# Moving the rotary part of the queries, its tables and the key rotation from the attention's start into the last column pair of the input projection (hybrid encoder, one core)

## The chip, the cores and the metric

One core of a Trainium2 chip runs the whole program. The metric is the device time of one execution in microseconds (us). The kernel before takes 1529.16 us, the median of three runs from 1528.39 to 1529.31.

## The reference

Two layers. Each normalises its input (512 positions of width 2048), projects it with one matrix `w_in`, and splits the result into three groups of heads and a gate. Cut to what matters here:

```python
cos, sin = rope_tables(positions)
for l in range(DEPTH):
    z = rmsnorm(x, pre_norm_g[l]) @ w_in[l]
    q_lat, kv_lat, k_pe, gb, gc, xin, q_mem, gate = split_cols(z)
    q = (rmsnorm(q_lat, q_norm_g[l]) @ w_uq[l]).reshape(b, s, 8, 192)
    q = concat([q[..., :128], apply_rope(q[..., 128:], cos, sin)], -1)
    k_pe = apply_rope(k_pe, cos, sin)                  # one key rotation, shared by the heads
    a_out = mla_attention(q, concat([k_nope, k_pe]), v)
    c_out = short_gated_conv(gb, gc, xin, conv_w[l])
    mem_n = rmsnorm(mem, mem_norm_g[l])                # 256 memory tokens
    m_out = memory_attention(q_mem, mem_n, w_mk[l], w_mv[l])
    y = concat([a_out, c_out, m_out], -1) * silu(gate)
    x = x + rmsnorm(y @ w_o[l], post_norm_g[l])
```

## The kernel before

Every product is made of three TensorE (PE) passes over a high and a low part of both operands (`mm3`, lines 243 to 247: L245, L246 and L247 are its three matmuls). So each block of weights that is loaded into a raw tile `wr` is first split: ScalarE (ACT) rounds it into `wh` (L172, or L177 with a gain), VectorE (DVE) takes the rest as `wl` (L173 or L178). What leaves PE and is to be multiplied again is split the same way by `split_to` (ACT L250, DVE L251). Raw tiles come from a pool of 8 buffers, `wh` and `wl` from 3 each, PSUM banks from 8, wide tiles ("slabs") from 19.

`Program` holds a list of steps. The order on PE, SyncE (SP, which issues the loads) and GpSimd (POOL, which issues accumulating loads) is the order of that list. The order on DVE and ACT is fixed at build time by a scheduler that starts from the same list. Each engine then runs its own list strictly in order; semaphores connect them. `pr.defer` puts a piece off until the steps have room for it.

A layer goes through these stages:

- The input projection, as five groups of two column blocks each (`gs[0]` to `gs[4]`), each group with seven products P1 to P7 in place of eight. A group's steps are four long (`c` = 0 to 3) per product. Between them stand small steps, such as `conv_turn`. Group 3 makes the latents (`lat`); group 4, the last, makes the gate columns `ga0` and `ga1`. Its 28 steps run P1, P5 with P2, P6 with P3, P7, P4.
- Within group 4: `latents_begin` normalises the latents, `latent_turn` transposes them (`cq`, `ckv`), `qm_turn` the memory queries (`Qm`), `gate_turn` the gate columns `gm` (a transpose on PE into a bank `tps`, then SiLU on ACT, L742). In layer 0 also `mem_rows` (L646): for each of two halves of the memory an ACT sum of squares over 128x2048 (L536), two small POOL operations for the root (L255, L257) and a DVE scaling (L544) give `mhs`.
- `mixer` (L1031). Layer 0: eight times `mem_turn` (PE transposes `mhs` into a bank `mps`, L660; ACT and DVE split it into `mH` and `mL`) alternates with the eight gate turns of `ga0` and `ga1` and with the memory keys and values (`mem_steps`: `mk` 24 matmuls of 256 columns and `mv` 12 of 512 columns for each of eight row pairs). The rotary tables (`tables`, L299, ropescr) and the key rotation (`k_rope`, L789) are deferred pieces beside these. Layer 1 fetches its memory keys and values, which were made earlier, and does the eight gate turns.
- Then the rotary part of the queries (`q_rope_steps`, L830): two product steps `prods` of 24 matmuls into four banks `qr`, whose weights are loaded from `w_uq` in pieces of 64 columns; four steps `rot`, each four DVE products against the tables (L856, L858), one DVE sum (L860) and one split into `qs`; four steps `turn`, each eight transposes on PE (`qrt`, L879) and two ACT copies into `QR` (L881). In layer 0 the products stand after the memory values, in layer 1 among the gate turns. `rot` and `turn` stand among the first steps of the attention.
- The attention as a software pipeline (L1011): scores (`sc`) on PE, maximum on DVE (L956), exponential and scaling on ACT (L959, L962), transposes `ptp` (L973), product with the values (`o`). First the four memory heads (their keys and values are `Km` and `Vm`), with the query, key and value projections of the first two heads (`qps`, `kps`, `vps`) between them; then the eight latent heads in pairs. The output projection follows.

Of the kernel before, what the change touches and what calls it, by code (L numbers as in the profile page):

```python
# [5 lines left out]
F32 = mybir.dt.float32  # L6
# [6 lines left out]
P = 128  # L13
# [64 lines left out]
class Program:  # L78
# [19 lines left out]
    def add(self, fn, units=(), room=0.0, ahead=None):  # L98

        self.steps.append((list(units), fn, room, self.ahead if ahead is None else ahead))  # L100
# [100 lines left out]
def encoder(tc, x, mem, positions, pre_norm_g, w_in, q_norm_g, w_uq, kv_norm_g, w_ukv, conv_w,  # L201
# [32 lines left out]
    def slab(name, dt=F32):  # L234
        return slabs.tile([P, D], dt, tag="slab", name=nm(name))
# [63 lines left out]
    def tables():  # L299
        n = NT * HALF  # L300
        v = {}

        def begin():
            v["scr"] = slab("ropescr").rearrange("p (i n) -> p i n", n=n)
            pf = const.tile([P, NT], F32, name="posf")
            nc.vector.tensor_copy(pf, G["posi"])
            ang, a2, tot = (v["scr"][:, i, :] for i in (0, 1, 4))
            for t in range(NT):
                nc.vector.tensor_scalar_mul(ang[:, t * HALF:(t + 1) * HALF], G["inv"], pf[:, t:t + 1])
            v["a1"] = scrap("ra1", n, F32R)  # L310
            nc.vector.tensor_copy(v["a1"], ang)
            nc.vector.tensor_tensor(a2, ang, v["a1"].bitcast(F32), op=ALU.subtract)
            v["ti"] = scrap("rti", n, I32)
            nc.vector.memset(tot, 0.0)

        def term(hi, part):
            def g():
                a2, f, tot = (v["scr"][:, i, :] for i in (1, 3, 4))
                a = v["a1"].bitcast(F32) if hi else a2
                nc.vector.tensor_scalar_mul(v["ti"], a, part)  # L320
                nc.vector.scalar_tensor_tensor(f, a, part, v["ti"], op0=ALU.mult, op1=ALU.subtract)
                nc.vector.tensor_tensor(tot, tot, f, op=ALU.add)
            return g

        def wave(shift):
            def g():
                q, f, tot, c = (v["scr"][:, i, :] for i in (2, 3, 4, 5))
                name = "cos2" if shift else "sin2"
                dst = G[name] = const.tile([P, NT, 2, HALF], F32, name=name)
                src = tot  # L330
                if shift:
                    nc.vector.tensor_scalar_add(q, tot, shift)
                    src = q
                nc.vector.tensor_scalar(f, src, MAGIC, None, op0=ALU.add)
                nc.vector.tensor_scalar(f, f, MAGIC, None, op0=ALU.subtract)
                nc.vector.tensor_tensor(f, src, f, op=ALU.subtract)
                nc.vector.tensor_scalar_mul(f, f, TWO_PI)
                nc.vector.tensor_scalar(f, f, PI_DOWN, -PI_DOWN, op0=ALU.min, op1=ALU.max)
                nc.scalar.activation(c, f, AF.Sin)
                c3 = c.rearrange("p (t i) -> p t i", i=HALF)  # L340
                if shift:
                    nc.vector.tensor_copy(dst[:, :, 0, :], c3)
                else:
                    nc.vector.tensor_scalar_mul(dst[:, :, 0, :], c3, -1.0)
                nc.vector.tensor_copy(dst[:, :, 1, :], c3)
            return g

        parts = inv_two_pi_parts(5)
        pr.defer(1.4, begin)
        for k in range(4, -1, -1):  # L350
            for hi in (False, True):
                pr.defer(0.8, term(hi, parts[k]))
        pr.defer(1.6, wave(0.0))
        pr.defer(1.8, wave(0.25))
# [673 lines left out]
            out.setdefault(int(n * start + k * n * (1 - start) / len(steps)), []).append(s)  # L1028
        return out

    def mixer(l, C, gates, pair2, tail):  # L1031

        prods, rot, turn = q_rope_steps(l)
        if l == 0:
            ms = [(f, u, 1.0) for f, u, _ in mem_steps(l)]
            add(tables)
            add(lambda: pr.defer(3.5, lambda: k_rope(C)))
            for q in range(8):
                add(lambda q=q: mem_turn(q))
                add(gates[q])  # L1040
                if q:
                    put(ms[2 * q - 2:2 * q])
            put(ms[14:])
            add(pr.settle)
            add(k_rope_turn)
            put(prods)
        else:
            add(mem_fetch)
            put([(g, []) for g in gates[:4]], prods[:1], [(g, []) for g in gates[4:]], prods[1:])
        sts = [{} for _ in range(4)]  # L1050
        qkv = qkv_steps(l, 0, sts[0])
        add(*rot[0])
        fill = []
        for t in range(NT):
            fill += [qkv[t]] + ([rot[t + 1]] if t + 1 < NT else []) + [turn[t]]
        its = [it for i in range(4) for it in mem_head(i)]
        m = len(its)
        between = spread(m, fill + qkv[4:])
        for pair in range(4):
            for i in range(2):  # L1060
                its += mla_head(2 * pair + i, sts[pair])
            nxt = tail if pair == 3 else spread(6 if pair == 2 else 8, qkv_steps(l, pair + 1, sts[pair + 1]))
            if pair == 2:
                nxt.update(pair2)
            for k, v in nxt.items():
                between[m + 8 * pair + k] = v
        pipeline(its, between)
# [144 lines left out]
    for l in range(depth):  # L1212
# [57 lines left out]
        put(a1, b1)  # L1270
        put(*gs[0][2:], *gs[1][2:])
        add(owns[2])
        put(gs[2][0])
        conv = [(conv_turn(l, c, C), []) for c in range(4)]
        put(weave(gs[2][1] + gs[2][2], conv, 2), *gs[2][3:])
        add(owns[3])
        put(*gs[3])
        add(owns[4])
        add(lambda l=l: latents_rows(l))
        if l == 0:  # L1280
            add(positions_load)
        g4 = [s for steps in gs[4] for s in steps]
        put(g4[:4])
        add(lambda l=l, C=C: latents_begin(l, C))
        put(g4[4:8])
        if l > 0:
            add(lambda C=C: k_rope(C))
        put(g4[8:16])
        if l == 0:
            add(mem_load)  # L1290
            G["mTd"] = dram.tile([4, P, D], F32, name="mTd")
        lat = [latent_turn("cq", j) for j in range(4)] + [latent_turn("ckv", j) for j in range(2)] + [k_rope_turn] * (l > 0)
        gm = lambda t, C=C: C["gm"][:, t, :]
        more = [(f, []) for f in lat + [qm_turn(j, C) for j in range(4)] + [gate_turn(12 + j, gm, j) for j in range(4)]]
        if l == 0:
            more.insert(8, (mem_rows, []))
        put(weave(g4[16:], more[:11], 1))
        put(more[11:])
        gates = [gate_turn(j, lambda t, C=C, j=j: C["ga0" if j < 4 else "ga1"][:, t, :], j % 4) for j in range(8)]
        G["left"] = Y = Left(False)  # L1300
        g0, g1, gains, fetch = out_proj(l)
# [7 lines left out]
        def sums(p):  # L1309
            def f():  # L1310
# [6 lines left out]

        last_pair = {0: [(sums(0), []), g0[0][0]], 1: [g0[0][1]], 2: [g0[0][2]], 3: [g0[0][3]],
                     4: [g1[0][0]], 5: [g1[0][1]], 6: [g1[0][2]], 7: [g1[0][3]]}
        mixer(l, C, gates, {6: [(use_y, []), (low(0), [])], 7: [(low(1), [])]}, last_pair)  # L1320
        add(sums(1))
        add(gains(0))
        put(*g0[1:])
# [47 lines left out]
```

## Time and profile before

| what | value |
|---|---|
| median of 3 runs | 1529.16 us |
| the profiled execution | 1529.26 us |
| its span, first to last instruction | 1527.5 us |
| mean granted TensorE clock | 0.994 |
| PE matmuls / PE weight loads busy | 98% / 84% of the span |
| DVE / ACT / POOL busy | 68% / 57% / 21% of the span |

The profile's times are of one execution, which the hardware profiler took. Some 1.8 us of its time lie outside the span. "Idle before" is the time that an engine stood still just before an instruction, with the instruction that released it. The ends of matmuls are modelled, since they overlap; the distance between two starts is the better measure of what a matmul costs.

### The profile page before, as it was taken

The numbers are of one execution on the slowest core, as the hardware profiler recorded it, in microseconds if no ns is written. First come the engines' busy times: TensorE is split into PE (matmuls) and PEld (weight loads), VectorE is DVE, ScalarE is ACT, GpSimd is POOL, SyncE is SP. The second block draws the span as 40 slices with busy tenths as digits, with TensorE's granted clock in tenths as the row PEclk, the third lists the DMA queues.
The fourth block names the chain that finished last, engine by engine and source line by source line (L and its number), as shares of the span: only waits on it lengthen the run. The fifth ranks groups of instructions, "written<-read, shape, count | busy, mean of one in ns | idle before, by whom it ended". The sixth has DMA issues, their size and how long they took to land.

```text
span 1527.5 us, 20239 instructions
## 1 busy us (share of the span) xinstructions
PE 1493.4 (98%) x7613; PEld 1281.3 (84%) x7613; DVE 1040.1 (68%) x1398; ACT 864.7 (57%) x1335; POOL 314.9 (21%) x313
## 2 busy tenths in 40 slices
PE   9999999999999999999999999999999999999996
PEld 7888888988898888888788888888988888888884
DVE  6965675565968668865778766675566586687656
ACT  7733534454768768645578434434454686775542
POOL 1233131332000000324320333131332000003231
PEclk9999999999999999999999999999999999999998
DMA  8999898989581112699997999897989411048895
GB/s 330 216 213 224 204 174 174 199 196 256 164 264 56 42 42 82 109 202 197 313 332 239 238 224 226 187 176 168 198 207 222 130 59 39 29 111 146 203 200 222
DMA packets 146934, 275.59 MB, mean 180 GB/s; under 512 B 17340, under 2 KB 40212, under 8 KB 143508
## 3 DMA queue, kind: packets, MB, share of 16 engines
q0 software_dynamic: 65600, 141.57, 48.5%
q1 hardware_dynamic: 81104, 132.68, 26.7%
q8 instruction: 59, 0.97, 0.3%
q14 instruction: 39, 0.32, 0.1%
q10 hardware_dynamic: 132, 0.05, 0.0%
HBM read 259.59 MB, written 14.68 MB: 180 GB/s over the span
## 4 chain that ended last, share of the span: by engine, by line
PE 85%; DVE 4%; DMA 3%; issue 3%; ACT 3%; POOL 2%; POOLq 0%; DVEq 0%; ACTq 0%
PE P L246 20%; PE P L247 20%; PE P L245 19%; PE ptp L973 2%; PE tps L731 1%; DMA mL<-mTd 1%; PE o L246 1%; PE sc L245 1%; PE mk L246 1%; PE sc L246 1%; PE sc L247 1%; PE mk L247 1%; PE o L247 1%; PE o L245 1%; DVE wl L173 1%
## 5 line engine op out<-in xcount | busy, mean ns | idle before, releaser
L173 DVE TENSOR_TENSOR wl<-wr,wh 128x1024 fp32r<-128x1024 f32 (+1 forms) x408 | 486.4, 1196 | 334.6 <-ACT wh L172 332.2
L172 ACT CAST wh<-wr 128x1024 fp32r<-128x1024 f32 (+1 forms) x408 | 420.6, 1033 | 482.5 <-PE P L247 418.2
L246 PE MATMUL P<-wl,S 128*128 128x512 f32 (+1 forms) x896 | 344.2, 384 | 2.8 <-DVE wl L173 2.8
L245 PE MATMUL P<-wh,S 128*128 128x512 f32 (+1 forms) x896 | 346.0, 386 | 0.0
L247 PE MATMUL P<-wh,S 128*128 128x512 f32 (+1 forms) x896 | 343.4, 383 | 0.0
L134 POOL DMA_DIRECT2D wr<-in_w_in_dram x160 | 193.4, 1209 | 484.5 <-DVE wl L173 365.2
L246 PE MATMUL P<-wl,A 128*128 128x512 f32 (+1 forms) x656 | 251.9, 384 | 2.1 <-DVE wl L173 2.1
L245 PE MATMUL P<-wh,A 128*128 128x512 f32 (+1 forms) x656 | 253.1, 386 | 0.2 <-ACT wh L172 0.2
L247 PE MATMUL P<-wh,A 128*128 128x512 f32 (+1 forms) x656 | 251.6, 384 | 0.5 <-DVE A L251 0.5
L246 PEld LDWEIGHTS P<-wl,S 128*128 128x128 f32 x896 | 168.3, 188 | 33.7 <-DVE wl L173 4.4
L247 PEld LDWEIGHTS P<-wh,S 128*128 128x128 f32 x896 | 168.2, 188 | 30.4
L245 PEld LDWEIGHTS P<-wh,S 128*128 128x128 f32 x896 | 168.1, 188 | 29.6 <-ACT wh L172 0.2
L134 POOL DMA_DIRECT2D wr<-in_w_o_dram x64 | 77.3, 1208 | 505.0 <-DVE rec L961 352.0
L246 PEld LDWEIGHTS P<-wl,A 128*128 128x128 f32 x656 | 123.2, 188 | 24.4 <-DVE wl L173 2.9
L247 PEld LDWEIGHTS P<-wh,A 128*128 128x128 f32 x656 | 123.1, 188 | 23.3 <-DVE A L251 1.2
L245 PEld LDWEIGHTS P<-wh,A 128*128 128x128 f32 x656 | 123.1, 188 | 22.3 <-ACT wh L172 0.6
L959 ACT ACTIVATE P<-sc,nm 128x512 f32<-128x512 f32 (+1 forms) x96 | 59.9, 624 | 36.4 <-DVE nm L956 35.8
L962 ACT ACTIVATE P<-P,rec 128x512 f32<-128x512 f32 (+1 forms) x96 | 62.1, 658 | 5.0 <-DVE rec L961 5.0
L956 DVE TENSOR_REDUCE nm<-sc 128x1 f32<-128x512 f32 (+1 forms) x96 | 57.2, 596 | 10.0 <-PE sc L954 6.3
L251 DVE TENSOR_TENSOR PT<-ptp,PT 128x512 fp32r<-128x512 f32 (+1 forms) x96 | 56.5, 594 | 8.5 <-ACT PT L250 8.1
L178 DVE SCALAR_TENSOR_TENSOR wl<-wr,cols,wh 128x512 fp32r<-128x512 f32 x64 | 46.2, 747 | 18.2 <-ACT wh L177 18.0
L177 ACT ACTIVATE wh<-wr,cols 128x512 fp32r<-128x512 f32 x64 | 44.2, 722 | 25.2 <-PE mk L246 10.9
(267 smaller groups left out, 2182.4 us busy)
## 6 DMA issues: line engine op xcount, KB each, us to landing
wr<-in_w_in_dram POOLq DMA_DIRECT2D x128, 512.0 KB, 6.9
wr<-in_w_in_dram SPq DMA_DIRECT2D x112, 512.0 KB, 5.6
wr<-in_w_o_dram POOLq DMA_DIRECT2D x64, 512.0 KB, 7.3
wr<-in_w_o_dram SPq DMA_DIRECT2D x48, 512.0 KB, 3.9
wr<-in_w_in_dram POOLq DMA_DIRECT2D x32, 416.0 KB, 5.4
wr<-in_w_in_dram SPq DMA_DIRECT2D x24, 416.0 KB, 4.3
wr<-in_w_mk_dram SPq DMA_DIRECT2D x16, 512.0 KB, 6.9
wr<-in_w_mv_dram SPq DMA_DIRECT2D x16, 512.0 KB, 4.5
```

The source lines that it names most:

```text
L134: engine.dma_start(dst, src, **kw)
L172: nc.scalar.copy(hi[:, :n], src)
L173: nc.vector.tensor_tensor(lo[:, :n], src, hi[:, :n].bitcast(F32), op=ALU.subtract)
L177: nc.scalar.activation(hi[:, h], src[:, h], AF.Copy, scale=g)
L178: nc.vector.scalar_tensor_tensor(lo[:, h], src[:, h], g, hi[:, h].bitcast(F32), op0=ALU.mult, op1=ALU.subtract)
L245: nc.tensor.matmul(ps, ah, bh, start=first, stop=False, **kw)
L246: nc.tensor.matmul(ps, ah, bl, start=False, stop=False, **kw)
L247: nc.tensor.matmul(ps, al, bh, start=False, stop=last, **kw)
L251: nc.vector.tensor_tensor(lo, src, hi.bitcast(F32), op=ALU.subtract)
L956: nc.vector.tensor_reduce(nmax, ps, axis=AX.X, op=ALU.max, negate=True)
L959: nc.scalar.activation(pt, ps, AF.Exp, bias=nmax, accum_out=tot)
L962: nc.scalar.activation(pt, pt, AF.Copy, scale=rec)
```

## The change

- The two products `prods` of the rotary queries now stand around the last step of P7 of group 4, the four `rot` steps between the steps of P4 and after them, alternating with the turns of the memory queries. Only `turn` stays in the attention.
- The tables are built beside group 3 in layer 0, from `positions` loaded one group earlier. The table's scratch is a raw tile now, no slab.
- The key rotation of layer 0 stands within group 4, as that of layer 1 did already; its transposes stand among the latent turns.
- In layer 0 `mem_rows`, which was put among the small steps before the gate turns of `gm`, is appended behind them.

```diff
@@ tables
-            v["scr"] = slab("ropescr").rearrange("p (i n) -> p i n", n=n)
+            v["scr"] = raw_p.tile([P, 1024], F32, tag="raw", name="ropescr")[:, :6 * n].rearrange("p (i n) -> p i n", n=n)
@@ mixer
-    def mixer(l, C, gates, pair2, tail):
-        prods, rot, turn = q_rope_steps(l)
+    def mixer(l, gates, turn, pair2, tail):
         if l == 0:
             ms = [(f, u, 1.0) for f, u, _ in mem_steps(l)]
-            add(tables)
-            add(lambda: pr.defer(3.5, lambda: k_rope(C)))
             for q in range(8):
                 add(lambda q=q: mem_turn(q))
                 add(gates[q])
                 if q:
                     put(ms[2 * q - 2:2 * q])
             put(ms[14:])
-            add(pr.settle)
-            add(k_rope_turn)
-            put(prods)
         else:
             add(mem_fetch)
-            put([(g, []) for g in gates[:4]], prods[:1], [(g, []) for g in gates[4:]], prods[1:])
+            put([(g, []) for g in gates])
...
-        add(*rot[0])
         fill = []
         for t in range(NT):
-            fill += [qkv[t]] + ([rot[t + 1]] if t + 1 < NT else []) + [turn[t]]
+            fill += [qkv[t], turn[t]]
@@ the layer loop
         add(owns[2])
+        if l == 0:
+            add(positions_load)
...
         add(owns[3])
+        if l == 0:
+            add(tables)
         put(*gs[3])
...
-        if l == 0:
-            add(positions_load)
...
-        if l > 0:
-            add(lambda C=C: k_rope(C))
+        add(lambda C=C: k_rope(C))
...
-        lat = [latent_turn("cq", j) for j in range(4)] + [latent_turn("ckv", j) for j in range(2)] + [k_rope_turn] * (l > 0)
+        lat = [latent_turn("cq", j) for j in range(4)] + [latent_turn("ckv", j) for j in range(2)] + [k_rope_turn]
...
+        prods, rot, qr_turn = q_rope_steps(l)
         if l == 0:
-            more.insert(8, (mem_rows, []))
-        put(weave(g4[16:], more[:11], 1))
-        put(more[11:])
+            more.append((mem_rows, []))
+        put(weave(g4[16:23], more[:7], 1), prods[:1], g4[23:24], prods[1:],
+            weave(g4[24:], [s for two in zip(rot, more[7:11]) for s in two], 1), more[11:])
```

The first place where the order differs is ACT's list at the end of group 4 in layer 0. `QmH` is the memory queries' high part, `y` from `tps` are SiLUs of gate turns, `mhs` from `mraw` is the sum of squares of a memory half, `mH` from `mps` the split of the transposed memory. Before:

```order
L763 ACTIVATE QmH_3073<-tps_3075 128x512
L536 ACTIVATE mhs_3129,st_3130<-mraw_2898 128x2048
L465 COPY ga_120_2565<-P_148_3008 128x512
L465 COPY ga_120_2565<-P_149_3009 128x512
L763 ACTIVATE QmH_3073<-tps_3104 128x512
L172 CAST wh_3113<-wr_2453 128x1024
L536 ACTIVATE mhs_3137,st_3138<-mraw_2900 128x2048
...
L742 ACTIVATE y_3224<-tps_3238 128x512
L250 CAST mH_3259<-mps_3261 128x512
```

And now, on the same engine at the same place of the program:

```order
L177 ACTIVATE wh_3471<-wr_3203,cols 128x512
L250 CAST qs_3335<-rm_3329 128x8x64
L763 ACTIVATE QmH_3300<-tps_3360 128x512
L763 ACTIVATE QmH_3300<-tps_3376 128x512
L763 ACTIVATE QmH_3300<-tps_3392 128x512
L742 ACTIVATE y_3404<-tps_3399 128x512
L742 ACTIVATE y_3404<-tps_3406 128x512
L742 ACTIVATE y_3404<-tps_3412 128x512
L742 ACTIVATE y_3404<-tps_3418 128x512
L536 ACTIVATE mhs_3424,st_3425<-mraw_2982 128x2048
L536 ACTIVATE mhs_3432,st_3433<-mraw_2984 128x2048
L250 CAST mH_3440<-mps_3442 128x512
```

The two sums of squares moved from among the steps of P7 and P4 to behind the last SiLU of `gm`, next to the split of the memory that they feed.

The second place is DVE's list around the first splits of the transposed memory (`mL`), in the same stage. `wl` from `wr` and `cols` are low parts of the memory's weights; `rm` from `qr` are rotation products. Before:

```order
L309 TENSOR_SCALAR ropescr_3244<-inv,posf 128x32 x4
L314 MEMSET ropescr_3244 128x128
L311 CAST ra_173_3251<-ropescr_3244 128x128
L178 SCALAR_TENSOR_TENSOR wl_3291<-wr_3055,cols,wh_3290 128x512
L312 TENSOR_TENSOR ropescr_3244<-ropescr_3244,ra_173_3251 128x128
L320 TENSOR_SCALAR rti_3254<-ropescr_3244 128x128
L321 SCALAR_TENSOR_TENSOR ropescr_3244<-ropescr_3244,rti_3254 128x128
L251 TENSOR_TENSOR mL_3260<-mps_3261,mH_3259 128x512
```

And now:

```order
L178 SCALAR_TENSOR_TENSOR wl_3472<-wr_3203,cols,wh_3471 128x512
L544 TENSOR_SCALAR mhs_3424<-mraw_2982,r_3429 128x2048
L544 TENSOR_SCALAR mhs_3432<-mraw_2984,r_3437 128x2048
L178 SCALAR_TENSOR_TENSOR wl_3472<-wr_3203,cols,wh_3471 128x512
L856 TENSOR_TENSOR rm_3367<-qr_3177,cos_2255 128x8x32
L858 TENSOR_TENSOR rm_3367<-qr_3177,sin_2228 128x8x32
L856 TENSOR_TENSOR rm_3367<-qr_3177,cos_2255 128x8x32
L858 TENSOR_TENSOR rm_3367<-qr_3177,sin_2228 128x8x32
L251 TENSOR_TENSOR mL_3441<-mps_3442,mH_3440 128x512
```

The small table operations are gone from here; the scalings of the memory and two of the four rotations now stand here, the third rotation ahead of the first `mL`.

The third place is DVE's list at the start of layer 0's attention, where `nm` is the maximum of a row of scores and `rec` the reciprocal of their sum. Before:

```order
L856 TENSOR_TENSOR rm_3954<-qr_3896,cos_3695 128x8x32
L858 TENSOR_TENSOR rm_3954<-qr_3896,sin_3619 128x8x32
L860 TENSOR_TENSOR rm_3954<-rm_3954 128x512
L251 TENSOR_TENSOR qs_3960<-rm_3954,qs_3960 128x8x64
L956 TENSOR_REDUCE nm_3967<-sc_3963 128x1
```

And now:

```order
L251 TENSOR_TENSOR Vm_3985<-mv_3481,Vm_3985 128x512
L956 TENSOR_REDUCE nm_3994<-sc_3990 128x1
L251 TENSOR_TENSOR Vm_3985<-mv_3482,Vm_3985 128x512
L173 TENSOR_TENSOR wl_4005<-wr_3806,wh_4004 128x1024
L961 RECIPROCAL rec_3999<-tot_3997 128x1
```

The rotations are gone from here, and the splits of the memory's values stand right at the first scores, where the rotary products lay between them before.

More of the change, by code (lines that the diff above doesn't have):

```diff
@@ L1319, in encoder @@
                      4: [g1[0][0]], 5: [g1[0][1]], 6: [g1[0][2]], 7: [g1[0][3]]}
-        mixer(l, C, gates, {6: [(use_y, []), (low(0), [])], 7: [(low(1), [])]}, last_pair)
+        mixer(l, gates, qr_turn, {6: [(use_y, []), (low(0), [])], 7: [(low(1), [])]}, last_pair)
         add(sums(1))
```

## The prediction

> **What bounds the kernel now.** I read the page first, then the stretches of 10 us by engine, then who waited for whom around the edited places, then single instructions in order of time.
>
> ```profile
> PE 1493.4 (98%) x7613; PEld 1281.3 (84%) x7613; DVE 1040.1 (68%) x1398; ACT 864.7 (57%) x1335; POOL 314.9 (21%) x313
> 470.00:480.00 10.00, 9.18 (x59) 7.60 (x58) 8.96 (x25) 9.88 (x28) 0.00 (x0) 1.00 0.00 0
> 480.00:490.00 10.00, 9.06 (x68) 7.79 (x67) 9.59 (x27) 8.74 (x28) 0.00 (x0) 1.00 0.33 99
> 1220.00:1230.00 10.00, 9.18 (x64) 7.72 (x63) 9.05 (x25) 9.88 (x27) 0.00 (x0) 1.00 0.00 1
> 1230.00:1240.00 10.00, 9.06 (x65) 7.66 (x64) 9.63 (x27) 8.74 (x28) 0.00 (x0) 1.00 0.24 75
> ```
>
> In a stretch's row stand its length, then busy us of PE, PEld, DVE, ACT and POOL, then the granted clock and the DMA share. PE is the bound: it is busy in 98% of the span, and the change leaves it the same matmuls. So the change can give back only PE's idle time, and can add idle time. Where the rotations stand now, at the start of each layer's attention, PE is idle for 0.82 + 0.94 = 1.76 us, with ACT and DVE near 9 of 10 us busy. Both layers together: 3.5 us. Two of the waits in layer 0's stretch show why:
>
> ```profile
> PE sc L245 <- DVE rm L858: 0.4, 1, 0.4
> PE o L246 <- DVE PT L251: 0.3, 1, 0.3
> ```
>
> The first is a score that waits for a bank until a rotation has read it. Everything else that the change touches lies beside a busy PE today, so its price is what it makes late.
>
> **The largest term: the memory's scaling, now behind the gate turns (layer 0).** The sum of squares of a memory half, its root and the scaling took, on ACT, POOL and DVE in turn:
>
> ```profile
> 385.83 1.91 ACT L536 ACTIVATE mhs<-mraw 128x2048 f32<-128x2048 f32 x1
> 387.63 0.19 ACT L536 ACTIVATION_READ_ACCUMULATOR mhs<-mraw 128x1 f32 x1
> 387.92 0.18 POOL L255 TENSOR_SCALAR ms<-st 128x1 f32<-128x1 f32 x1 [16.25 <-ACT mhs L536]
> 388.19 0.57 POOL L257 TENSOR_TENSOR r<-ms,mhalf 128x1 f32<-128x1 f32 x1
> 388.79 1.29 DVE L544 TENSOR_SCALAR mhs<-mraw,r 128x2048 f32<-128x2048 f32 x1 [0.30 <-POOL r L257]
> 393.41 1.29 DVE L544 TENSOR_SCALAR mhs<-mraw,r 128x2048 f32<-128x2048 f32 x1 [1.59 <-ACT wh L172]
> ```
>
> ACT is held for 387.82 - 385.83 = 2.0 us per half, and from there to the scaled rows it takes 390.08 - 387.82 = 2.3 us more. All this was over at some 395 us, well before PE came to the first memory transposes:
>
> ```profile
> 399.23 0.39 PE L246 MATMUL P<-wl,A 128*128 128x512 f32 x1
> 399.46 0.39 PE L247 MATMUL P<-wh,A 128*128 128x512 f32 x1
> 399.69 1.91 PE L731 MATMUL tps<-identr,gm 128*128 128x128 f32 x16
> 401.44 0.60 PE L660 MATMUL mps<-identr,mhs 128*128 128x128 f32 x4
> 399.89 0.72 ACT L177 ACTIVATE wh<-wr,cols 128x512 fp32r<-128x512 f32 x1 [1.36 <-PE P L247]
> 400.52 2.04 ACT L742 ACTIVATE y<-tps 128x512 f32<-128x512 f32 x4
> ```
>
> Starts of 512-column matmuls are 0.23 us apart, four transposes take 1.75 / 4 = 0.44, one SiLU 0.51. In the new order both sums of squares stand behind the last SiLU of `gm`, and that SiLU waits for PE's last `gm` transposes. PE's very next instruction needs both scaled halves, so nothing covers this chain. Count from the end of P4. PE does seven turns (three of `Qm`, four of `gm`): 7 x 0.44 = 3.1 us. ACT has half a weight block (0.72), one `qs` copy (0.62, row below) and seven copies of 0.51: 4.9 us. Then two sums of squares, 4.0, and 2.3 for the second half's root and scaling: 11.2 us. PE stands from 3.1 to 11.2. **I take 8.0 us**; 6.8 if ACT is only one SiLU behind PE (0.5 + 4.0 + 2.3), 8.6 if it is later still. POOL has nothing queued ahead there.
>
> **What is queued behind the scaling on DVE.** DVE works in order, and in the new list half a weight split, the four products of the third rotation and only then the first `mL` follow the scaling.
>
> ```profile
> L178 DVE SCALAR_TENSOR_TENSOR wl<-wr,cols,wh 128x512 fp32r<-128x512 f32 x14 | 10.1, 746 | 0.0
> L251 DVE TENSOR_TENSOR mL<-mps,mH 128x512 fp32r<-128x512 f32 x4 | 2.7, 684 | 0.0
> L856 DVE TENSOR_TENSOR rm<-qr,cos 128x256 f32<-128x256 f32 x8 | 3.3, 415 | 0.1
> L858 DVE TENSOR_TENSOR rm<-qr,sin 128x256 f32<-128x256 f32 x8 | 3.3, 412 | 0.0
> L860 DVE TENSOR_TENSOR rm<-rm 128x512 f32<-128x512 f32 x4 | 2.7, 682 | 0.0
> L251 DVE TENSOR_TENSOR qs<-rm,qs 128x512 fp32r<-128x512 f32 x4 | 2.8, 690 | 1.3 <-ACT qs L250 1.3
> L250 ACT CAST qs<-rm 128x512 fp32r<-128x512 f32 x4 | 2.5, 623 | 3.8 <-DVE rm L860 3.8
> 403.83 0.39 PE L246 MATMUL mk<-mL,wh 128*128 128x256 f32 x1 [0.35 <-DVE mL L251]
> ```
>
> That is 0.75 + 4 x 0.41 + 0.68 = 3.1 us, against 1.75 us of transposes on PE: a wait of up to 1.3 for the second `mk` matmul, where 0.35 is waited now. Successive DVE instructions overlap a little; I take 1.0, so **+0.65** (0 to 1). The gate transpose before the second row pair takes the bank of the fourth `qr` tile and so waits for the fourth rotation. From the end of the first `mk`: two ACT halves 1.4, a DVE half 0.75, `qs` 0.69, four products 1.65, together 4.5 us, while PE has 12 x 0.23 + 0.44 = 3.2 us of work. **+1.1** (0 to 1.4). After that DVE's backlog is gone. This is also where the change does not do all that it says: two of the four rotations end in the memory stage.
>
> **The clock after the wait.** The trace has one like case, at the start of layer 1: PE waits 3.2 us for a memory load.
>
> ```profile
> 765.92 0.58 PE L246 MATMUL mk<-mL,wh 128*128 128x256 f32 x1 [3.23 <-DMA mL<-mTd]
> 766.30 0.42 PE L247 MATMUL mk<-mH,wl 128*128 128x256 f32 x1
> 766.51 0.41 PE L245 MATMUL mk<-mH,wh 128*128 128x256 f32 x1
> 404.18 0.28 PE L245 MATMUL mk<-mH,wh 128*128 128x256 f32 x1
> 404.30 0.28 PE L246 MATMUL mk<-mL,wh 128*128 128x256 f32 x1
> 764.50:765.00 0.50, 0.00 (x0) 0.00 (x0) 0.50 (x2) 0.50 (x1) 0.00 (x0) 0.71 0.93 254
> 771.00:771.50 0.50, 0.50 (x4) 0.50 (x4) 0.00 (x0) 0.48 (x1) 0.00 (x0) 0.50 1.02 414
> 771.50:772.00 0.50, 0.50 (x5) 0.45 (x4) 0.22 (x1) 0.50 (x2) 0.00 (x0) 0.96 1.05 422
> ```
>
> The granted clock drops to a half about 2 us into the wait and comes back at 771.5, 5.6 us after PE resumed. Meanwhile `mk` starts are 0.21 us apart, not 0.12: 44% of the time is lost. Here PE's first 2.7 us after the wait are set by DVE's `mL` anyway, so the loss falls on the 2.9 us that follow: **+1.3** (0.3 if the clock is back after some 3.4 us, 2.5 if all 5.6 us count).
>
> [...]
>
> **What is gained at the attention.** Per layer 4 x (4 x 0.41 + 0.68 + 0.69) = 12 us of DVE and 2.5 us of ACT leave the stretch whose PE idle time is 1.76. But cover leaves too: in layer 0 the 48 rope products (11 us of PE) stood between the splits of the memory's keys and values and the first scores; now those splits and the first scores meet. I take **-1.0** of 1.76 for layer 0 (-1.76 to +1.5). In layer 1 fifteen turns now stand in a row: PE 15 x 0.44 = 6.6 us, ACT 15 x 0.51 = 7.7 plus two `qs` copies; banks run out and PE waits about a microsecond, and ACT starts the attention late. **0** (-1.76 to +2.2).
>
> **What costs nothing, and what hides it.**
>
> ```profile
> L173 DVE TENSOR_TENSOR wl<-wr,wh 128x832 fp32r<-128x832 f32 x9 | 9.2, 1025 | 10.1 <-ACT wh L172 10.1
> L322 DVE TENSOR_TENSOR ropescr<-ropescr 128x128 f32<-128x128 f32 x10 | 2.9, 290 | 0.3
> 330.00:340.00 10.00, 8.96 (x40) 7.09 (x39) 8.28 (x12) 3.18 (x4) 3.79 (x3) 1.00 0.78 175
> 1130.00:1140.00 10.00, 8.96 (x40) 7.10 (x39) 8.97 (x14) 3.16 (x3) 3.60 (x3) 1.00 0.60 146
> ```
>
> The tables: some 40 operations of up to 0.29 us, about 10 us, in group 3, where DVE stands 10.1 us against 9.2 us of nine splits (the first row, 255 to 275 us). They about fill it, two steps of split weights ahead cover the rest: 0, up to 1 without that cover. The key rotation: layer 1 has it in group 4 already, and both layers lose the same 1.04 us there: 0. The four `w_uq` loads and `positions` pass SP's queue earlier, in front of the memory rows: 0, since eight steps lie between issue and use.
>
> **The sum.** 8.0 + 0.65 + 1.1 + 1.3 - 1.0 + 0 = +10.0 us on the profiled execution's 1529.26: 1539.3. The median of the runs is 0.1 us lower: **1539.2 us**. Ends: all low 6.8 + 0 + 0 + 0.3 - 1.76 - 1.76 = +3.6, 1532.8; high 8.6 + 1 + 1.4 + 2.5 + 1.5 + 2.2 = +17, 1546.
>
> **Rivals.**
>
> *Faster, because the memory scaling is covered after all and the attention's waits go.* Then -3.5: 1525.7. The price rests on the four stretches above. It decides from the point at which the chain costs PE less than 3.5 us. Against it: the two sums of squares alone are 4.0 us of one engine behind PE's own last transposes. 3%.
>
> *The memory's weights come late.* The four `qs` tiles now hold half of the eight raw buffers until the attention, so the loads of `mk` and `mv` cycle through four.
>
> ```profile
> wr<-in_w_mk_dram SPq DMA_DIRECT2D x16, 512.0 KB, 6.9
> ```
>
> A row pair takes 24 x 0.12 + 12 x 0.23 + 0.88 = 6.5 us on PE, four buffers last for two pairs, 13 us; landing takes 6.9 and some 2.5 (an estimate: a half of `wh`, a half of `wl` and a queue of one such step) go before the split that frees a buffer. Loads of over 10.5 us would stall PE, a few times by 1 us or so: +3, 1542. 10%.
>
> *Layer 1 pays at its crowded turns*: +2.2, 1541.4. For it: ACT is the busier engine there. Against it: the scores need no gate. 8%.
>
> *No change that can be told*: a measurement of this kernel tells about 0.2%, 3.1 us. It needs all low ends and half a microsecond more: 3%.
>
> The forecast has 76%; I call 1533.5 to 1545 the range, which takes in both later rivals and leaves out the corners. Slower by over 0.2%: 94%, within 3%, faster 3%.
>
> **What would show it.** Right: in layer 0 PE waits about 8 us at `mps` for DVE's `mhs` (L544), the granted clock halves there, and a `tps` waits for `rm` (L858); PE's idle time at layer 0's attention start shrinks. A wait at `mps` under 4 us, or a clock that stays full, would make the sum wrong; waits of the memory's `wh` for DMA would speak for the second rival.

## The result, and the profile after

The changed kernel took 1538.36 us (median of 6 runs, 1536.98 to 1541.47) against 1529.24 us before (6 runs, 1528.39 to 1530.14). The ratio is 1.006, with a 95% interval of 1.005 to 1.007: slower by 7.6 to 10.7 us. The profiled execution has a span of 1538.4 us against 1527.5.

PE's busy time is the page's first number, and the list of who waited for whom gives total us, times and the longest. Both are of the changed kernel:

```profile
PE 1494.8 (97%) x7613; PEld 1283.1 (83%) x7613; DVE 1042.0 (68%) x1398; ACT 864.0 (56%) x1335; POOL 316.6 (21%) x313
```

```profile
PE mps L660 <- DVE mhs L544: 7.0, 2, 5.5
...
PE tps L731 <- DVE rm L858: 1.8, 1, 1.8
...
PE ptp L973 <- ACT P L959: 1.2, 3, 0.6
...
PE tps L731 <- ACT y L742: 1.0, 1, 1.0
PE sc L245 <- ACT P L959: 0.8, 1, 0.8
```

PE has the same 7613 matmuls and nearly the same busy time; its idle time grew. The first two waits are new and stand in layer 0's memory stage. No wait for a memory weight (`mk` or `mv` for DMA of layer 0) is among them. The waits for `rm` at a score (0.8 us before) are gone. In layer 1 a wait for a `y` copy is new, and the waits for `P` have grown: before they were 0.7 at `ptp` and 0.4 at `sc`.

To see which stage lost what, take two instructions per layer that both kernels run with the same wait ahead of them: one in group 4, behind the tables and the key rotation's products but ahead of everything else that the change moves, and one in the attention. The first starts no later than before. The kernel before, then the changed one:

```profile
335.15 0.50 PE L246 MATMUL P<-wl,S 128*128 128x512 f32 x1 [1.04 <-DVE wl L173]
626.88 0.39 PE L246 MATMUL o<-PT,V 128*128 128x256 f32 x1 [0.70 <-DVE PT L251]
1134.99 0.50 PE L246 MATMUL P<-wl,S 128*128 128x512 f32 x1 [1.04 <-DVE wl L173]
1377.62 0.39 PE L246 MATMUL o<-PT,V 128*128 128x256 f32 x1 [0.70 <-DVE PT L251]
```

```profile
334.41 0.50 PE L246 MATMUL P<-wl,S 128*128 128x512 f32 x1 [1.03 <-DVE wl L173]
635.13 0.39 PE L246 MATMUL o<-PT,V 128*128 128x256 f32 x1 [0.70 <-DVE PT L251]
1143.41 0.50 PE L246 MATMUL P<-wl,S 128*128 128x512 f32 x1 [1.04 <-DVE wl L173]
1386.53 0.39 PE L246 MATMUL o<-PT,V 128*128 128x256 f32 x1 [0.70 <-DVE PT L251]
```

Layer 0's stretch went from 626.88 - 335.15 = 291.7 to 300.7 us: +9.0. Layer 1's went from 242.6 to 243.1: +0.5. Together +9.5, which agrees with the timed +9.1. What the span shows beyond that lies in stretches that the change doesn't touch; the end of layer 1 alone, from the fourth row to the first `P<-T4h`, took 126.3 us before and between 126.4 and 132.1 in the later runs.

The place of the loss, in order of time, in the changed kernel:

```profile
410.53 2.25 PE L731 MATMUL tps<-identr,gm 128*128 128x128 f32 x16
412.00 2.07 ACT L742 ACTIVATE y<-tps 128x512 f32<-128x512 f32 x4
413.91 1.96 ACT L536 ACTIVATE mhs<-mraw 128x2048 f32<-128x2048 f32 x1
415.80 1.96 ACT L536 ACTIVATE mhs<-mraw 128x2048 f32<-128x2048 f32 x1
416.93 1.29 DVE L544 TENSOR_SCALAR mhs<-mraw,r 128x2048 f32<-128x2048 f32 x1 [3.01 <-POOL r L257]
418.27 0.47 PE L660 MATMUL mps<-identr,mhs 128*128 128x128 f32 x1 [5.49 <-DVE mhs L544]
418.94 1.29 DVE L544 TENSOR_SCALAR mhs<-mraw,r 128x2048 f32<-128x2048 f32 x1 [0.73 <-POOL r L257]
420.29 0.90 PE L660 MATMUL mps<-identr,mhs 128*128 128x128 f32 x3 [1.54 <-DVE mhs L544]
427.02 0.40 PE L245 MATMUL mv<-wh,mH 128*128 128x512 f32 x1
432.16 0.66 PE L731 MATMUL tps<-identr,ga 128*128 128x128 f32 x4 [1.79 <-DVE rm L858]
```

ACT's two sums of squares begin when the last SiLU of `gm` ends; the second half of the memory is scaled at 420.2. PE finished the gate transposes at 412.8, does one transpose of the first half in between, and is idle for 5.49 + 1.54 = 7.0 us in all. The last row is the gate turn that waits for the fourth rotation.

### The profile page after: what moved, and what is told of

It reads as the page before. It is cut to its first block, busy times and chain, and to the rows that moved or that the text cites. A ratio compares the mean times of both kernels' runs of the same rounds, so it can differ in the third digit from the quotient of the medians.

```text
span 1538.4 us, 20259 instructions
## 1 busy us (share of the span) xinstructions
PE 1494.8 (97%) x7613; PEld 1283.1 (83%) x7613; DVE 1042.0 (68%) x1398; ACT 864.0 (56%) x1335; POOL 316.6 (21%) x313
## 4 chain that ended last, share of the span: by engine, by line
PE 83%; DVE 4%; DMA 4%; ACT 3%; issue 3%; POOL 2%; POOLq 0%; DVEq 0%; ACTq 0%
PE P L246 19%; PE P L247 19%; PE P L245 19%; PE ptp L973 2%; POOL wr L134 2%; PE tps L731 1%; DMA mL<-mTd 1%; DMA wr<-in_w_o_dram 1%; DVE wl L173 1%; PE o L246 1%; PE sc L245 1%; PE sc L246 1%; PE sc L247 1%; PE o L247 1%; PE o L245 1%
```

## The experiments

Each run's own numbers stand in this table: the median (the kernel before took 1529.24 beside the changed kernel, 1529.05 beside the next eight, 1529.73 beside the two after them and 1528.82 beside the last two), the ratio with its interval where there is more than one run, and the two stretches between the rows above, in us. Layer 1's stretch repeats within 0.1 us in all six profiles in which it is as before, so the stretches tell more than the medians, whose intervals are some 0.1% to either side. Layer 0's is less certain: in layer1_only, whose layer 0 has the order of before, it took 292.7, not 291.7.

| kernel | median | ratio (95%) | layer 0 | layer 1 |
|---|---|---|---|---|
| before | 1529.24 | | 291.7 | 242.6 |
| changed | 1538.36 | 1.006 (1.005 to 1.007) | 300.7 | 243.1 |
| rows_early | 1531.22 | 1.0012 (1.0001 to 1.0023) | 291.9 | 243.1 |
| rows_late | 1537.44 | 1.0056 (1.0043 to 1.0069) | 300.2 | 242.7 |
| layer1_only | 1531.76 | 1.0012 (1.0004 to 1.0021) | 292.7 | 243.1 |
| tables_key | 1529.78 | 1.0004 (0.9995 to 1.0013) | 291.7 | 242.6 |
| clock_fill | 1541.69 (one) | | 299.6 | 243.2 |
| half_squares | 1539.09 (one) | | 299.2 | 243.2 |
| l0_gates | 1529.21 | 0.9998 (0.9989 to 1.0006) | 291.4 | 242.6 |
| both_gates | 1530.16 | 1.0005 (0.9996 to 1.0014) | 291.5 | 243.2 |
| rot_ahead | 1531.82 | 1.0013 (1.0003 to 1.0023) | 293.9 | 242.6 |
| rows_p4 | 1532.21 (one) | | 294.1 | 243.2 |
| l0_ahead | 1527.39 | 0.9993 (0.9984 to 1.0002) | 289.9 | 242.6 |
| both_ahead | 1528.78 | 1.0001 (0.9992 to 1.0010) | 289.9 | 241.8 |

### rows_early: the scaling put back ahead

```
-        if l == 0:
-            more.append((mem_rows, []))
...
-        put(weave(g4[16:23], more[:7], 1), prods[:1], g4[23:24], prods[1:],
+        put(weave(g4[16:23], more[:7], 1), prods[:1], [(mem_rows, [])] * (l == 0), g4[23:24], prods[1:],
```

> The changed kernel with one thing put back: the memory's scaling (mem_rows) stands between the two products of the queries' rope part, ahead of the last pair of P4, not behind the gate turns. Theory (the wait at mps and its clock loss make nearly all of the loss, 7.0 + 1.6 us in the trace of the changed kernel): 1538.4 - 8.6, plus up to 0.7 for a wait for the first mL that the slow clock hid, so 1529.5 to 1531; no wait for mhs, full clock from 400 to 440 us, the wait of a tps for rm (L858) stays at 1.5 to 2 us. Rival (the loads of the memory's weights, the tables or the rotations carry a good part of the loss): 1534 or more, with a new wait in the memory stage.

Measured: layer 0 is 8.8 us shorter than in the changed kernel, the wait for `mhs` is gone, the clock stays at 1.00 from 410 to 440 us and the wait for `rm` stays at 1.78 us. The median, 1531.2, lies just above the 1529.5 to 1531 expected and far from 1534. So the place of the scaling carries nearly all of the loss; loads, tables and rotations don't.

### rows_late: the scaling alone moved behind the gate turns

```
-            more.insert(8, (mem_rows, []))
-        put(weave(g4[16:], more[:11], 1))
-        put(more[11:])
+            more.append((mem_rows, []))
+        put(weave(g4[16:], more[:10 + (l > 0)], 1))
+        put(more[10 + (l > 0):])
```

> The kernel before with one part of the change alone: the memory's scaling stands behind the gate turns of gm; rope part, tables and key rotation stay at the attention. Theory (the chain of sums of squares, root and scaling behind the last SiLU costs by itself): a wait of 6.5 to 7.5 us at mps, a granted clock of 0.5 within it, together 8 to 9 us: 1537 to 1538.5. Rival (the chain is exposed only because the rotations fill ACT and DVE beside it): a wait under 3 us, under 1532.5.

Measured: +0.56%, 8.5 us (6.6 to 10.6). The waits on PE in this kernel:

```profile
PE mps L660 <- DVE ropescr L309: 5.2, 1, 5.2
...
PE mps L660 <- DVE mhs L544: 1.5, 1, 1.5
```

The first is the same wait under another name: DVE's `ropescr` piece, which `mps` doesn't read, is the instruction behind the scaling, and the event is put down to it. In all 6.7 us, with the clock at 0.50 within it. One part of the change, alone, makes the loss that the whole change makes; the rotations beside it aren't needed for it.

### layer1_only and tables_key: the other parts alone

```
-            put([(g, []) for g in gates[:4]], prods[:1], [(g, []) for g in gates[4:]], prods[1:])
+            put([(g, []) for g in gates])
...
+            put(weave(g4[16:23], more[:7], 1), prods[:1], g4[23:24], prods[1:],
+                weave(g4[24:], [s for two in zip(rot, more[7:11]) for s in two], 1), more[11:])
```

(for layer 1 only), and, in the other kernel,

```
-            add(tables)
-            add(lambda: pr.defer(3.5, lambda: k_rope(C)))
...
         add(owns[3])
+        if l == 0:
+            add(tables)
...
-        if l > 0:
-            add(lambda C=C: k_rope(C))
+        add(lambda C=C: k_rope(C))
```

> The kernel before with the rope part of the queries moved in layer 1 alone, where no memory scaling stands in the way; layer 0 as before. Theory: the waits at the attention's start (1.6 us) give way to waits in the row of gate turns, and the two about cancel: 1529.2 to 1530. Rival one (crowded turns): 1531.4. Rival two (the waits at the attention go and nothing takes their place): 1527.5.

> The kernel before with only the tables, the positions' load and layer 0's key rotation moved into the projection (the scratch of the tables in a raw buffer); the queries' rope part stays at the attention, the memory's scaling one place later in the same row of turns. Theory: covered on both sides, 1529 to 1529.5. Rivals: a step of split weights comes late in group 3 (+1, 1530.2); or DVE freed in layer 0's memory stage is worth something (1528.2 or less).

The tables and the key rotation cost nothing that can be told: both stretches are as before, the first begins at 334.9 us where it began at 335.1, and the ratio is 1.0004 (0.9995 to 1.0013). Layer 1's part makes its own stretch 0.5 us longer, in this run and in the six others that have it in this order, with the waits that the changed kernel shows (1.0 for `y`, 0.8 and 1.2 for `P`). The timed ratio says more, 1.8 us (0.6 to 3.2), and the median, 1531.8, misses the 1529.2 to 1530 expected and lies near the first rival's 1531.4. In the profiled execution layer 0, whose order is as before, lost 1.0 by a later `mL`; whether that comes with the change or by chance stays open, and so does layer 1's price in time beyond the 0.5.

### clock_fill: what the halved clock costs

```
-            more.append((mem_rows, []))
+            more += [(mem_rows, []), (lambda: warm(45), [])]
```

> The changed kernel with 45 transposes of the identity (45 x 0.11 = 5 us of work that nobody reads) put on PE between the gate turns and the first memory transposes, in the hole of 5.5 us. Theory: the wait for the scaling itself stays (the second half still comes at about 420.3), but the granted clock stays full through the memory stage; the stretch from there to the first mv shrinks from 6.7 us to about 5.5, and a wait of about 0.9 for the first mL (L251) appears, which the slow clock had hidden. In all -1.2 us. Rival (the slow matmuls after the wait come from something else, say the weights' splits): the stretch stays at 6.7 us.

Measured: layer 0 is 1.2 us shorter than in the changed kernel, the clock stays full (1.00 from 414 to 426 us), and the `mL` wait appears:

```profile
413.01 5.13 PE L1172 MATMUL warm<-identr 128*128 128x128 f32 x45
420.63 0.55 PE L660 MATMUL mps<-identr,mhs 128*128 128x128 f32 x3 [1.68 <-DVE mhs L544]
423.33 0.39 PE L246 MATMUL mk<-mL,wh 128*128 128x256 f32 x1 [0.73 <-DVE mL L251]
426.19 0.40 PE L245 MATMUL mv<-wh,mH 128*128 128x512 f32 x1
```

From the second half's transposes to the first `mv` it takes 426.19 - 420.63 = 5.6 us, where the changed kernel took 427.02 - 420.29 = 6.7. So the clock's net price is some 1.2 us, and it hid 0.7 of waiting for `mL`. The single time of the run, 1541.7, doesn't show the gain: its end of layer 1, where nothing differs, took 132.1 us.

### half_squares: half of the squares

```
-            normalise_rows(G.pop(f"mraw{t}"), hs)
+            xt, h = G.pop(f"mraw{t}"), D // 2
+            r = row_factor(xt[:, :h], hs[:, :h])
+            nc.vector.tensor_scalar_mul(hs, xt, r)
```

> The changed kernel with each sum of squares of the memory taken over 1024 of its 2048 columns (it leaves out half of the squares, so the scaling is another). Theory (ACT's two sums of squares, root and scaling stand in series behind the last SiLU): each square takes 1.0 us instead of 2.0, the second half of the memory comes 2.0 us earlier, PE's idle time at mps falls from 7.0 to 5.0, and the clock still halves, since PE stands for over 3 us in one piece: layer 0 is 2.0 us shorter. Rival (the chain waits for something beside ACT, a load of the memory or a free buffer): less than 1 us.

This kernel leaves out half of the squares. The expectation was missed: layer 0 is 1.6 us shorter, not 2.0, and only 0.8 of it is PE's wait (6.2 against 7.0). ACT's two sums took 1.7 us less from the start of the first to the end of the second, but the chain then ran into another link (in this kernel the scaling is L651):

```profile
415.45 1.10 ACT L536 ACTIVATE mhs<-mraw 128x1024 f32<-128x1024 f32 x1
415.71 0.18 POOL L255 TENSOR_SCALAR ms<-st 128x1 f32<-128x1 f32 x1 [46.84 <-ACT mhs L536]
416.58 1.29 DVE L651 TENSOR_SCALAR mhs<-mraw,r 128x2048 f32<-128x2048 f32 x1 [2.15 <-POOL r L257]
416.73 1.18 POOL L255 TENSOR_SCALAR ms<-st 128x1 f32<-128x1 f32 x1 [0.18 <-ACT mhs L536]
418.00 0.56 POOL L257 TENSOR_TENSOR r<-ms,mhalf 128x1 f32<-128x1 f32 x1
418.59 1.28 DVE L651 TENSOR_SCALAR mhs<-mraw,r 128x2048 f32<-128x2048 f32 x1 [0.72 <-POOL r L257]
```

POOL's second `ms` takes 1.18 us where the first took 0.18, and ends just behind DVE's scaling of the first half. So here the root of the second half comes only behind the scaling of the first. That ACT is in the chain holds, that it is the whole chain does not. The rest of the gain, 0.7, fits the clock: PE worked 3.1 us at half speed after the wait, not 4.6 (the times are below), and 44% of the 1.5 us between is 0.7. That a stand of over 3 us is needed for the halving isn't shown: the one here was 4.7, but 2.3 in rot_ahead (below) brought it too.

### l0_gates and both_gates: the gate turn that waits for a rotation

```
                 add(lambda q=q: mem_turn(q))
-                add(gates[q])
                 if q:
                     put(ms[2 * q - 2:2 * q])
+                add(gates[q])
```

on top of the scaling put back, with layer 1 as before in the first kernel and moved in the second.

> The rope part moved in layer 0 alone (layer 1 as before), the memory's scaling between the two products, and in the memory stage each gate turn placed behind the products of its row pair, not ahead of them, so that the turn that needs the bank of the fourth qr tile comes 6 us later. Theory: the wait of a tps for rm (L858), 1.8 us, goes; the first mk comes 0.4 earlier and waits up to 0.4 more for mL; layer 0 is 1.2 to 1.8 us shorter than with the scaling put back alone, 1527.4 to 1528.0 in all, against 1529.0 before. Rival (another turn then takes that bank and waits, or mk does): 1529 or more, with a wait of over 1 us in the memory stage.

> The same as the run with the gate turns behind their products, but with the rope part moved in layer 1 too, as in the changed kernel. Theory: layer 1 costs 0.5 us (243.1 against 242.6 us between the same two instructions), so 1527.9 to 1528.5. Rival (layer 1's part costs as much as the run with layer 1 alone timed, 1 to 3 us): 1529 to 1530.5.

The wait for `rm` is gone, but the rival holds in part: now a memory transpose waits 0.9 us for a bank that a `y` copy still holds, and the first `mk` 0.4 for `mH`. Layer 0 is 0.5 us shorter than with the scaling put back alone, not 1.2 to 1.8, and the time is that of before. Between the two kernels layer 1's part again shows 0.5 us in its stretch (243.2 against 242.6); in the medians it is 0.95, and both_gates, at 1530.2, lies above the 1527.9 to 1528.5 expected and within its rival's 1529 to 1530.5.

### rot_ahead, rows_p4: earlier rotations, a halfway place for the scaling

```
-        put(weave(g4[16:23], more[:7], 1), prods[:1], g4[23:24], prods[1:],
-            weave(g4[24:], [s for two in zip(rot, more[7:11]) for s in two], 1), more[11:])
+            put(weave(g4[16:23], more[:7], 1), prods[:1], [(mem_rows, [])], g4[23:24], more[7:8], prods[1:], rot[:1],
+                g4[24:25], more[8:9], rot[1:2], g4[25:26], more[9:10], rot[2:3], g4[26:27], more[10:11], rot[3:],
+                g4[27:], more[11:])
```

for layer 0 alone; and, in the other kernel, the changed one with `mem_rows` behind the first pair of `zip(rot, more[7:11])`.

> The rope part moved in layer 0 alone (layer 1 as before), the memory's scaling between the two products, the gate turns where the changed kernel has them, and the rotations one step earlier each: the first right behind the second product, the next two behind the next two steps of P4, the fourth behind the third, the turns of Qm ahead of them. Theory (the tps waits only because the fourth rotation stands too late on DVE): the wait for rm (L858) goes and layer 0 is about 1.5 us shorter than with the scaling put back alone (291.9 to about 290.4 us between the two instructions at 335 and 627 us), 1527.5 to 1528 in all. Rival (DVE has no room before the memory stage: four rotations of 3.0 us beside the splits of P4's weights): PE waits for wl in P4 by 1 us or more, and nothing is won.

> The changed kernel with the memory's scaling in the middle of the last P4 (behind its second step of four and the first turn of Qm), 5.5 us ahead of its end, so that the chain of sums, roots and scalings begins some 8 us ahead of the first mps. Theory (only where the chain stands decides): the wait for mhs is gone or under 1 us and the clock stays full; ACT, with 6.3 us of work in the 8.6 us up to the gate turns' SiLUs, gets 4.0 more and is late by about 2 there, so the first mL or the gates' turns wait 0.5 to 2 us more than with the scaling put back to its old place. Rival (the change's placement makes the loads or POOL late, not the chain): a wait of over 3 us remains.

In rot_ahead neither the gain nor the rival came: layer 0 is 2.0 us longer than with the scaling put back alone. The memory stage did lose its wait for `rm`, and no `wl` was late, but the turn of `Qm` that I had put ahead of the second product found no free bank:

```profile
394.77 1.19 ACT L465 COPY ga<-P 128x512 f32<-128x512 f32 x2 [0.56 <-DVE ga L460]
395.41 1.11 PE L731 MATMUL tps<-identr,qm 128*128 128x128 f32 x4 [2.29 <-ACT ga L465]
396.18 0.78 PE L245 MATMUL qr<-wh,cqH 128*128 128x512 f32 x1
```

It waited 2.3 us for a read of `P`, and the clock fell to a half there for 3.4 us: one wait for a bank in place of the one removed.

In rows_p4 the wait for `mhs` is gone and the clock stays full (`mk` starts are 0.12 us apart), as expected, and ACT and DVE are late: PE waits 1.2 us for ACT's `y` and 0.5 for DVE's `ga` in the row of gate turns, 0.7 for the first `mL`, and 1.6 for a bank that another `mL` has yet to read. Layer 0 is 2.2 us longer than in rows_early, a little over the 0.5 to 2 expected. So the scaling needs a place where ACT and DVE are free, not only an early one.

### l0_ahead, both_ahead: the order mended

```
-            put(weave(g4[16:23], more[:7], 1), prods[:1], [(mem_rows, [])], g4[23:24], more[7:8], prods[1:], rot[:1],
-                g4[24:25], more[8:9], rot[1:2], g4[25:26], more[9:10], rot[2:3], g4[26:27], more[10:11], rot[3:],
-                g4[27:], more[11:])
+            put(weave(g4[16:23], more[:7], 1), prods[:1], [(mem_rows, [])], g4[23:24], prods[1:], rot[:1],
+                g4[24:25], more[7:8], rot[1:2], g4[25:26], more[8:9], rot[2:3], g4[26:27], more[9:10], rot[3:],
+                g4[27:], more[10:])
```

> As the run with the rotations one step earlier each, but the first turn of Qm only behind the first rotation and one step of P4, when a rotation has given a bank back; layer 1 as before. Theory (what that run lost were 2.3 us of waiting for a bank at the first turn of Qm and the halved clock behind it, and its rotations no longer delay the memory stage): no wait over 0.5 us between 335 and 627 us, full clock, layer 0 in 290.1 to 290.5 us against 291.7 before, 1527.7 to 1528.3 in all. Rival (the splits of P4's weights come late beside four rotations): waits for wl of 1 us or more, layer 0 at 291.5 or more.

> The whole change in that order: rope part moved in both layers, the memory's scaling between the two products of layer 0. Theory: layer 0 as in the run with layer 0 alone (290.1 to 290.5); in layer 1 the row of turns is three shorter, since the turns of Qm stand ahead of the gates of gm, so the wait for a y copy (1.0 us) shrinks, 242.6 to 243.0 us against 242.6 before; 1527.9 to 1528.7 in all. Rival (a bank or ACT comes late in layer 1 as it did): 243.1 or more.

Layer 0 takes 289.9 us in both, 1.8 less than before and a little under the 290.1 to 290.5 expected, with no wait over 0.35 us in the memory stage and the memory heads. That is what moving the rope part is worth there once nothing else is made late. With layer 1 in the same order its stretch is 241.8, 0.8 us shorter than before, where 242.6 to 243.0 were expected: the wait for `y` is gone, though one `ptp` now waits 1.3 for `P`. The medians are 1527.4 and 1528.8 against 1528.8, the ratios 0.9993 (0.9984 to 1.0002) and 1.0001 (0.9992 to 1.0010): the gains in the stretches are below what the timing can tell, and in both_ahead's profile the end of layer 1, which nobody touched, took 2.3 us more than before. Faster than the kernel before is likely for l0_ahead, but not shown.

## Why the prediction was right

Forecast 1539.2, measured 1538.4, by the mechanism that carried it. Point by point:

- **The memory's scaling, 8.0 (6.8 to 8.6): 7.0.** The chain was right: from the end of P4 at 409.2 to the second half's transposes at 420.29 are 11.1 us, 11.2 by my count. The count of PE's side was short: its turns took 3.6 us, not 3.1, since the last ones waited 0.36 for a bank that a `QmL` split had yet to read, and one transpose of the first half ran inside the wait (0.47). That it is this chain, and its place alone, is shown by rows_early and rows_late.
- **First `mL` and the clock, 0.65 + 1.3: 2.1 together** (from the end of the `gm` transposes to the first `mv` it took 401.60 to 406.69 before and 412.78 to 427.02 now: 9.15 us lost, 7.0 of them the wait; 0.47 of the 2.1 is the transpose inside it), but not as I split it. The halved clock made PE so slow that it never waited for `mL`; clock_fill brought that wait back, 0.73. A recovery of 3.4 us, from which the clock's low end of 0.3 was worked out, is shown as a fixed time by no run: from PE's restart to the full clock it took 5.6 us at layer 1's start before, 4.6 here (from the second half's transposes, 420.29 to 424.91), 3.9 in layer1_only (766.99 to 770.87) and 3.3 in rot_ahead (395.41 to 398.72).
- **The fourth rotation, 1.1 (0 to 1.4): 1.8**, outside its bounds. The count left out ACT's cast of `qs`, ahead of which DVE stands 0.69 us idle.
- **Layer 0's attention, -1.0 (-1.76 to +1.5): -2.4**, outside its bounds. PE has the same work from the first score to the row at `o` in both kernels: 626.88 - 465.69 = 161.2 us before, 635.13 - 476.39 = 158.7 now, and 158.8 in rows_early and l0_ahead. No new conflict with the memory's splits came. My lower end was the idle time of two stretches of 10 us; the gain is not limited to them. Ahead of the first score 11.4 us were lost: 9.15 and 1.8 as above, and 0.5 that my sum has no term for (0.3 in group 4, 0.2 in the memory stage). The first scores, before and now:

```profile
465.69 0.28 PE L245 MATMUL sc<-Km,QmH 128*128 128x256 f32 x1
476.39 0.28 PE L245 MATMUL sc<-Km,QmH 128*128 128x256 f32 x1
```

- **Layer 1, 0: +0.5.** The row of turns did wait for ACT, 1.0 us, which is what layer 1 lost ahead of its first score; behind it 0.5 was gained, in spite of waits for `P`.
- **Tables, key rotation, SP's queue, 0: 0.** The memory's rows were issued at 371.7 us, not 347.5, and nobody waited for them, with the scaling put back ahead neither. In the changed kernel's stretches DVE fills up with the tables while PE stays full; the key rotation's products run on DVE from 314.9 to 320.2 beside a full PE, and the stretch with its split, the last row, has PE at 8.96 as before:

```profile
250.00:260.00 10.00, 10.00 (x52) 9.32 (x51) 9.62 (x29) 3.56 (x4) 4.84 (x4) 1.00 0.80 131
260.00:270.00 10.00, 10.00 (x55) 9.92 (x54) 7.75 (x21) 5.40 (x9) 2.76 (x3) 1.00 0.95 179
310.00:320.00 10.00, 10.00 (x52) 9.40 (x51) 7.28 (x19) 8.29 (x21) 2.63 (x3) 1.00 0.85 219
330.00:340.00 10.00, 8.96 (x40) 7.07 (x40) 8.52 (x13) 3.20 (x4) 3.05 (x3) 1.00 0.59 143
```

- **The rivals.** Late weights of the memory: layer 0's memory stage shows no wait for a load in any of these profiles. The one on the fast side failed at the point that I gave it: the chain cost 7.0, not under 3.5. Crowded turns in layer 1: the kind was right, +0.5 where I gave 2.2.

The five terms miss by -1.0, +0.15, +0.7, -1.4 and +0.5, and 0.5 had no term. The chain at `mps`, the largest part, was forecast by its mechanism and nearly by its size; that the sum of the stretches, +9.5 against +10.0, is better than its parts is luck, since the misses cancel.

## What to carry to other kernels

When a step is appended to the end of a row "because it is used next", count its chain over all engines backward from its use: here 4 us of ACT and 2.3 us of POOL and DVE, behind 5 us that ACT already owed. Put it where ACT and DVE are idle, and check each moved step for the bank that it needs and the bank that it gives back. A gain of 2 us at a stage that PE bounds to 98% is easily smaller than what its new place makes late.

## What the hardware showed that I had not expected

**The clock changed on a fixed beat in these profiles.** The rows give the stretch and, third from the end, the granted clock; where a row's value lies between 1.00 and 0.50, it gives the moment of the change. The changed kernel (the hole in layer 0, then the layer boundary), rows_late, half_squares and rot_ahead:

```profile
414.50:415.00 0.50, 0.00 (x0) 0.00 (x0) 0.00 (x0) 0.50 (x1) 0.00 (x0) 0.67 0.27 102
424.50:425.00 0.50, 0.50 (x5) 0.50 (x5) 0.00 (x0) 0.01 (x1) 0.00 (x0) 0.59 0.00 0
776.00:776.50 0.50, 0.50 (x7) 0.50 (x6) 0.50 (x1) 0.50 (x1) 0.00 (x0) 0.98 1.02 414
779.50:780.00 0.50, 0.50 (x4) 0.50 (x3) 0.00 (x0) 0.50 (x1) 0.00 (x0) 0.60 1.03 397
```

```profile
405.00:405.50 0.50, 0.00 (x0) 0.00 (x0) 0.45 (x1) 0.50 (x1) 0.02 (x1) 0.91 0.00 0
412.00:412.50 0.50, 0.50 (x5) 0.50 (x4) 0.50 (x2) 0.50 (x1) 0.00 (x0) 0.76 0.35 135
```

```profile
416.00:416.50 0.50, 0.00 (x0) 0.00 (x0) 0.00 (x0) 0.50 (x3) 0.50 (x1) 0.66 0.00 0
422.50:423.00 0.50, 0.50 (x5) 0.50 (x4) 0.50 (x2) 0.42 (x1) 0.00 (x0) 0.51 0.00 0
```

```profile
395.00:395.50 0.50, 0.09 (x1) 0.09 (x2) 0.50 (x2) 0.49 (x2) 0.00 (x0) 0.81 0.00 0
398.50:399.00 0.50, 0.50 (x3) 0.46 (x2) 0.00 (x0) 0.00 (x0) 0.00 (x0) 0.78 0.00 0
```

A mean of 0.67 over half a microsecond is 0.17 at full clock and the rest at half, so it fell at 414.67; 0.59 gives 424.91. Low times: 10.2 us, then 776.48 to 779.90, 3.4; in rows_late 405.41 to 412.24, 6.8; in half_squares 416.16 to 422.99, 6.8; in rot_ahead 395.31 to 398.72, 3.4. All are one, two or three times 3.4, together 30.73, nine times 3.414. These two falls of the changed kernel lie 361.81 us apart; its falls at 762.83 and 1513.76, found in the same way, lie 348.16 and 1099.09 us behind the first. 361.81 / 106, 348.16 / 102 and 1099.09 / 322 all give 3.413. The length of a wait alone did not set what it cost by the clock: 2.3 us of waiting brought 3.4 us at half, waits of 6.2 to 7.0 us brought 6.8 or 10.2. That its place on the beat decides is my estimate from these times; no run tests it alone. The plainest pair is the case that I read in the prediction, layer 1's first `mL`. There PE waited 3.23 us, and the clock was at a half from 764.71 to 771.54, 6.8 us. In layer1_only PE waits 3.22 us for the same tile:

```profile
766.99 0.39 PE L246 MATMUL mk<-mL,wh 128*128 128x256 f32 x1 [3.22 <-DMA mL<-mTd]
767.00:767.50 0.50, 0.50 (x4) 0.50 (x5) 0.50 (x1) 0.40 (x1) 0.00 (x0) 0.96 0.98 389
770.50:771.00 0.50, 0.50 (x5) 0.50 (x5) 0.00 (x0) 0.00 (x0) 0.00 (x0) 0.63 1.04 406
```

Here the clock is at a half from 767.46 to 770.87, 3.4 us, and all of it behind the wait. My 5.6 us of recovery, read off one case, were no constant.

**POOL's `ms` took longer beside DVE's scaling.** It took 0.18 us alone and 1.18 when issued beside DVE's scaling (half_squares, above); in the changed kernel, where the two meet from 417.94 to 418.22 us, it took 0.33. Both times it ended just behind the scaling: at 417.91 against 417.87, and at 418.27 against 418.22. What delayed it no row shows.
